# Up-projection of a convolutional feed-forward block: column blocks of 384 without overlap, edge taps from the preceding PSUM bank

## The chip, the core and the metric

The kernel runs on one core of one Trainium2 chip. The metric is the device time of one execution in microseconds (us). TensorE multiplies a loaded 128x128 weight tile by a moving operand of up to 512 columns and writes to PSUM, eight banks of 512 fp32 columns in each of 128 partitions. ScalarE, VectorE and GpSimd work on tiles beside it; each engine takes its own instructions strictly in order. The profile calls the engines PE, ACT, DVE and POOL, and SP is the engine that issues the transfers.

## The reference

Two layers, each a mixer (sliding-window or chunk-band attention) and a channel mixer, each closed by a layer norm. The change lies in the channel mixer, which the reference computes so:

```
def conv_ffn(h, prev, w_up, conv_w, conv_b, w_down):
    u = h @ w_up
    B, T, C = u.shape
    ...
    ue = jnp.concatenate([prev.astype(u.dtype), u], axis=1)
    y = conv_b
    for tap in range(CONV_W):
        y = y + conv_w[tap] * ue[:, tap:tap + T]
    a, g = jnp.split(y, 2, axis=-1)
    out = (jax.nn.gelu(g) * a) @ w_down
    return out, ue[:, T:]
```

There are 1024 prompt positions and 8 sample sequences of 16 positions, so 1152 positions in all, 1024 model channels and 2 x 2816 up-projected channels. The convolution is causal with three taps: a position needs the up-projected values of the two positions before it. For the prompt the first two positions see zeros; for a sample sequence they see rows of a stored state.

## The kernel before

All large products run in split fp32: each operand is a high and a low part, and three products (low by high, high by low, high by high) are summed in PSUM. H holds the modulated input of the channel mixer, transposed (channels on partitions, 1152 positions as columns), as a high and a low part; `wh` and `wl` are the two parts of a weight chunk.

The up-projection goes through 44 chunks of 128 channels a layer: chunk j of the value half (gg = 0) and chunk j + 22 of the gate half (gg = 1). Each chunk makes three position blocks, bi = 0, 1, 2. One block is 24 matmuls in line 266 (`mmT`: eight with `wl`, sixteen with `wh`) into one PSUM bank of the ring `ub` (banks 0, 1, 2). In the table `UB` (L995) block 0 takes columns 0 to 383, and blocks 1 and 2 take 388 columns that begin four columns before their own 384, so that all taps of a block find their inputs in the block's own bank.

`conv` (L972) then works on the bank: ScalarE writes bias plus the third tap to a tile `y` in SBUF (L975), and VectorE adds the other two taps straight from PSUM (L978), two instructions of 384 columns, or in block 2 two of 256 (prompt) and two on the sample part. GpSimd adds the sample state (L993). For the gate half follow gelu on ScalarE (L1022), the product with the value half on GpSimd (L1024) and the split of the result into X (ScalarE's cast in L151, VectorE's subtraction in L162). The down-projection (L1049, banks 3, 4, 5) multiplies two chunks of activations by two chunks of weights, and VectorE adds each result to `acc` (L1040). Up-blocks and down-blocks alternate.

The last chunk pair is made in `down_last` (L1053), block by block between the last down-projection rows, with `pregate` (L1104) before it: VectorE and GpSimd scale `acc` and add the residual (L1108, L1109).

Code order gives the dependences; a scheduler with a model of the engines' times then sets the order of the instructions on every engine at build time. Accesses of different engines to one PSUM bank are kept apart as whole banks, not as columns: a matmul group that writes bank 0 waits for every earlier reader of bank 0.

At the start of a channel mixer the last token tile, tile 7 of positions 896 to 1023, is still in its layer norm (`norm_tail`, L852): VectorE normalises it (L856), TensorE transposes it (L866, eight matmuls into banks 6 and 7), ScalarE applies the modulation (L878, eight copies), and ScalarE and VectorE split it into H. Block 2 needs this tile, blocks 0 and 1 do not. Tile names: F is a large SBUF arena (among others `y`, `acts`), C holds small per-position values, PS is PSUM.

Of the kernel before, what the change touches and what calls it, by code (L numbers as in the profile page):

```python
# [12 lines left out]
AF = mybir.ActivationFunctionType  # L13
# [6 lines left out]
NFF = 22  # L20
BLK = ((0, 384), (384, 384), (768, 384))
# [67 lines left out]
class Trunk:  # L89
# [693 lines left out]
    def ln_region(self):  # L783
        fa = Arena(self.F)
        x = fa.take(2048)
        self.xring = Ring([x[:, i * 1024 : i * 1024 + 1024] for i in range(2)])
        y = Arena(x)
        self.yg = y.ring(2, 384)
        self.at = y.ring(2, 384)
        for k in ("hf", "xr", "tmp"):  # L790
            setattr(self, k, fa.take(1024))
        self.E = fa.take(704)
        self.cw = fa.take(176)
        self.uo = [fa.take(198) for _ in range(2)]
        for k in ("gateS", "gateP", "lng", "lnb"):
            setattr(self, k, fa.take(1024))
        y = fa.take(1152)
        self.ya = Ring([y[:, i * 384 : i * 384 + 384] for i in range(3)])
        self.zt = fa.take(1024)
        assert fa.o <= self.NF, fa.o  # L800

    def ln_consts(self, l, i):
# [139 lines left out]
    def ffn(self, l, xsrc, xdst, affs):  # L942
        nc, I, O, H = self.nc, self.I, self.O, self.H
# [25 lines left out]
        x2b = self.x2p.tile([128, 768], F32R, name=f"x2ffn{l}", tag="x2b")  # L969
        aring = Ring([(x2.take(384), x2.take(384)) for _ in range(5)] + [(x2b[:, 0:384], x2b[:, 384:768])])  # L970

        def conv(ps, cc, bi, y):  # L972
            w = lambda i: cw[:, cc, i : i + 1]
            off = 0 if bi == 0 else 4
            nc.scalar.activation(y, ps[:, off : off + 384], AF.Identity, bias=w(3), scale=w(2))  # L975

            def tap(o, u, i):
                nc.vector.scalar_tensor_tensor(o, u, w(i), o, op0=ALU.mult, op1=ALU.add)  # L978

            if bi == 0:  # L980
                tap(y[:, 1:384], ps[:, 0:383], 1)
                tap(y[:, 2:384], ps[:, 0:382], 0)
            elif bi == 1:
                tap(y, ps[:, 3:387], 1)
                tap(y, ps[:, 2:386], 0)
            else:
                tap(y[:, 0:256], ps[:, 3:259], 1)
                tap(y[:, 0:256], ps[:, 2:258], 0)
                ys = y[:, 256:384].rearrange("p (s q) -> p s q", q=16)
                us = ps[:, 260:388].rearrange("p (s q) -> p s q", q=16)  # L990
                tap(ys[:, :, 1:16], us[:, :, 0:15], 1)
                tap(ys[:, :, 2:16], us[:, :, 0:14], 0)
                nc.gpsimd.tensor_add(ys[:, :, 0:2], ys[:, :, 0:2], E4[:, cc])  # L993

        UB = ((0, 384), (380, 388), (764, 388))  # L995

        acts = {}
        ya = {}

        def up(j, gg):  # L1000
            w = self.wload(I["wup"][l, j + 22 * gg])
            for bi in range(3):
                up_block(w, j, gg, bi)

        def up_block(w, j, gg, bi):
            cc = j + 22 * gg
            s0, n = UB[bi]
            ps = self.bank(ub.next())
            self.mmT(w, ps, s0, n)
            if gg == 0:  # L1010
                y = ya[bi] = self.ya.next()
            else:
                y = self.yg.next()
            conv(ps, cc, bi, y)
            if bi == 2:
                uo = self.uo[gg].rearrange("p (j s r) -> p j s r", s=9, r=2)
                src = ps[:, 258:402].rearrange("p (s q) -> p s q", q=16)[:, :, 0:2]
                nc.scalar.copy(uo[:, j % 11], src)
                if j % 11 == 10:
                    nc.sync.dma_start(O["conv"][l, gg, j // 11], self.uo[gg])  # L1020
            if gg == 1:
                nc.scalar.activation(y, y, AF.Gelu_apprx_tanh)  # L1022
                a = self.at.next()
                nc.gpsimd.tensor_mul(a, y, ya[bi])  # L1024
                h, lo = aring.next()
                self.split(a, h, lo, "a", "v")
                acts[(j, bi)] = (h, lo)
# [25 lines left out]
        def down_last():  # L1053

            js = (NFF - 2, NFF - 1)
            wu = [self.wload(I["wup"][l, NFF - 1 + 22 * gg]) for gg in range(2)]
            wr, wg = [], []
            for j, y in zip(js, (self.tmp, self.hf)):
                s = self.ws.next()
                wr.append(s)  # L1060
                nc.sync.dma_start(s, I["wdn"][l, j])
                nc.gpsimd.tensor_mul(y, s, self.gateP)
                wg.append(self.wring.next())
                self.split(y, *wg[-1], "a", "v")
            hfr = Ring([self.hf, self.tmp])
            for t in LO[l]:
                for bi in UP[l].get(t, ()):
                    for gg in range(2):
                        up_block(wu[gg], NFF - 1, gg, bi)
                    if bi == 2:  # L1070
                        w = [self.wring.next() for _ in range(2)]
                        for s, x in zip(wr, w):
                            self.split(s, *x, "a", "v")
                row = acc[:, t * 1024 : t * 1024 + 1024]
                sm = self.sm.next()
                for hf in range(2):
                    n = slice(hf * 512, hf * 512 + 512)
                    ps = dmm(js, wg if t < 8 else w, t, n)
                    if t == 8:
                        nc.vector.tensor_mul(self.tmp[:, n], ps, self.gateS[:, n])  # L1080
                        ps = self.tmp[:, n]
# [43 lines left out]
        self.step(0)  # L1125
        affs = affs()
        down_last()


# [214 lines left out]
```

## Time and profile before

| | |
|---|---|
| median of three runs | 2989.72 us (2989.35 to 2991.23) |
| the profiled execution | 2989.4 us |
| its span, first to last instruction | 2987.6 us |
| PE busy | 2858.9 us, 96% |
| PE weight loads | 2546.9 us, 85% |
| DVE busy | 1537.8 us, 51% |
| ACT busy | 1146.0 us, 38% |
| POOL busy | 913.8 us, 31% |
| channel mixer of layer 0, first up-block | at 516.81 us |
| channel mixer of layer 1, first up-block | at 2122.80 us |

A row of the timeline gives the start, the length, the engine, the line and the operation of a run of like instructions, and in brackets how long the engine had been idle and what it waited for. A matmul's own length holds its passage through the array, so that neighbours overlap: what a row of matmuls costs is read from its start to the start of the next row. Idle time of an engine that nothing waits for costs nothing.

### The profile page before, as it was taken

How to read it: one execution, taken by the hardware profiler on the slowest of the kernel's cores; microseconds unless marked ns; L12 is line 12 of the kernel's file. 1: busy time of each engine (PE TensorE's matmuls, PEld its weight loads, DVE VectorE, ACT ScalarE, POOL GpSimd, SP SyncE). 2: the span in 40 equal slices, each digit the busy share in tenths (PEclk: the TensorE clock that was granted, in tenths of full speed). 3: DMA queues.
4: the chain of work that ended last, by engine and by line, in shares of the span. 5: the costliest groups of instructions: out<-in, count | busy, mean ns of one | idle time of the engine just before them, and what ended most of it. 6: DMA issues, size and time to landing. Idle time of an engine off the chain costs nothing.

```text
span 2987.6 us, 43232 instructions
## 1 busy us (share of the span) xinstructions
PE 2858.9 (96%) x16582; PEld 2546.9 (85%) x16582; DVE 1537.8 (51%) x3416; ACT 1146.0 (38%) x2432; POOL 913.8 (31%) x661
## 2 busy tenths in 40 slices
PE   6999889999999999998999999989999999999996
PEld 4886668898888898997899888867899999999995
DVE  4365678424444344358412777766724444444468
ACT  2465644332222222224434666652442222222224
POOL 3122333323222222354551121221422222222253
PEclk8999999999999999999999999999999999999998
DMA  8545353622222312223785467673311111111121
GB/s 298 186 150 164 109 161 121 231 70 92 78 88 81 102 64 86 82 71 109 272 297 174 126 152 192 183 215 118 126 49 43 42 38 44 43 43 43 41 80 73
DMA packets 175967, 353.95 MB, mean 118 GB/s; under 512 B 34680, under 2 KB 91832, under 8 KB 175504
## 3 DMA queue, kind: packets, MB, share of 16 engines
q1 hardware_dynamic: 175760, 351.19, 36.6%
q8 instruction: 130, 2.13, 0.3%
q14 instruction: 77, 0.63, 0.1%
HBM read 285.22 MB, written 75.35 MB: 121 GB/s over the span
## 4 chain that ended last, share of the span: by engine, by line
PE 78%; DVE 8%; DMA 4%; ACT 3%; issue 2%; POOL 2%; SPq 0%; DVEq 0%; ACTq 0%; POOLq 0%
PE PS L266 45%; PE PS L1049 16%; PE PS L278 8%; PE PS L210 2%; PE PS L551 2%; PE PS L532 2%; PE PS L506 1%; DVE F L472 1%; PE PS L509 1%; DMA F<-in_adaw_dram 1%; DVE acc L1109 1%; DMA ws<-oN 1%; POOL wl L162 1%; DVE F L938 1%; DMA ws<-in_adaw_dram 1%
## 5 line engine op out<-in xcount | busy, mean ns | idle before, releaser
L266 PE MATMUL PS<-H,wh 128*128 128x384 f32 (+1 forms) x5472 | 1044.9, 338 | 0.0
L266 PEld LDWEIGHTS PS<-H,wh 128*128 128x128 f32 x5472 | 965.3, 188 | 17.7 <-issue 7.5
L162 POOL TENSOR_TENSOR wl<-ws,wh 128x1024 fp32r<-128x1024 f32 x167 | 405.5, 2433 | 743.4 <-ACT wh L151 696.9
L978 DVE SCALAR_TENSOR_TENSOR F<-PS,F 128x256 f32<-128x256 f32 (+2 forms) x704 | 353.0, 512 | 536.5 <-ACT F L975 523.2
L266 PE MATMUL PS<-H,wl 128*128 128x384 f32 (+1 forms) x2736 | 566.7, 344 | 21.1 <-POOL wl L162 9.4
L266 PEld LDWEIGHTS PS<-H,wl 128*128 128x128 f32 x2736 | 489.4, 190 | 53.3 <-issue 15.7
L975 ACT ACTIVATE F<-PS,F 128x384 f32<-128x384 f32 x264 | 177.5, 672 | 750.7 <-PE PS L266 749.3
L1049 PE MATMUL PS<-wh,X 128*128 128x512 f32 x1320 | 412.0, 394 | 9.6 <-DVE acc L1040 4.1
L1040 DVE TENSOR_TENSOR acc<-acc,PS 128x512 f32<-128x512 f32 x324 | 221.5, 686 | 270.9 <-PE PS L1049 270.3
L1024 POOL TENSOR_TENSOR F<-F 128x384 f32<-128x384 f32 x132 | 138.1, 1046 | 650.6 <-ACT F L1022 648.7
L1049 PEld LDWEIGHTS PS<-wh,X 128*128 128x128 f32 x1320 | 245.5, 188 | 63.0 <-issue 6.7
L151 ACT CAST wh<-ws 128x1024 fp32r<-128x1024 f32 x174 | 180.0, 1045 | 165.7 <-PE PS L1049 75.9
L1049 PE MATMUL PS<-wl,X 128*128 128x512 f32 x660 | 216.5, 393 | 0.0
L278 PE MATMUL PS<-wh,H 128*128 128x256 f32 (+1 forms) x936 | 171.2, 312 | 6.2 <-DVE H L162 5.4
L278 PEld LDWEIGHTS PS<-wh,H 128*128 128x128 f32 x936 | 136.0, 193 | 16.6 <-DVE H L162 6.0
L1049 PEld LDWEIGHTS PS<-wl,X 128*128 128x128 f32 x660 | 124.1, 188 | 28.1
L588 POOL TENSOR_TENSOR F<-F,x2att 64x512 f32<-64x512 f32 x62 | 79.4, 1280 | 216.2 <-DVE F L563 146.8
L162 DVE TENSOR_TENSOR X<-F,X 128x384 fp32r<-128x384 f32 x110 | 96.9, 881 | 88.9 <-ACT X L151 88.5
L532 PE MATMUL PS<-C,F 128*128 128x128 f32 x720 | 117.6, 284 | 16.0 <-DVE wh L538 7.6
L278 PE MATMUL PS<-x1att,H 128*128 128x512 f32 x504 | 131.9, 403 | 0.0
L1022 ACT ACTIVATE F<-F 128x384 f32<-128x384 f32 x132 | 69.2, 524 | 143.4 <-DVE F L978 129.2
L532 PEld LDWEIGHTS PS<-C,F 128*128 128x128 f32 x720 | 83.0, 143 | 37.9 <-DVE wh L538 11.0
(211 smaller groups left out, 3494.4 us busy)
## 6 DMA issues: line engine op xcount, KB each, us to landing
ws<-in_wup_dram SPq DMA_DIRECT2D x88, 512.0 KB
F<-in_adaw_dram SPq DMA_DIRECT2D x74, 512.0 KB
ws<-in_wdn_dram SPq DMA_DIRECT2D x44, 512.0 KB
ws<-in_adaw_dram SPq DMA_DIRECT2D x32, 512.0 KB
x1att<-kH SPq DMA_DIRECT2D x60, 256.0 KB
xd<-F SPq DMA_DIRECT2D x27, 512.0 KB
F<-xd SPq DMA_DIRECT2D x27, 512.0 KB
vH<-X SPq DMA_DIRECT2D x40, 256.0 KB
```

The lines of the kernel that those rows point to most:

```text
L151: nc.scalar.copy(out, in_)
L162: self.eng(el).tensor_sub(lo, src, hi.bitcast(F32))
L266: self.nc.tensor.matmul(out[:, 0:n], w[a][:, k * 128 : k * 128 + 128], H[:, p, k, s0 : s0 + n], start=i == 0, stop=i == 23)
L278: self.nc.tensor.matmul(out[:, 0:n], H[:, p, j * kn + k, t0 : t0 + 128], w[a][:, k * n : k * n + n], start=i == 0, stop=i == 23,)
L532: nc.tensor.transpose(t[:, m * 128 : m * 128 + 128], p[:, (kt - k0) * 128 : (kt - k0) * 128 + 128], self.ident)
L588: self.eng("v" if last else "p").tensor_mul(on[r, q], on[r, q], rb[r, :])
L975: nc.scalar.activation(y, ps[:, off : off + 384], AF.Identity, bias=w(3), scale=w(2))
L978: nc.vector.scalar_tensor_tensor(o, u, w(i), o, op0=ALU.mult, op1=ALU.add)
L1022: nc.scalar.activation(y, y, AF.Gelu_apprx_tanh)
L1024: nc.gpsimd.tensor_mul(a, y, ya[bi])
L1040: nc.vector.tensor_add(row[:, n], row[:, n], ps)
L1049: nc.tensor.matmul(ps, ac[m][p][:, cs], w[m][q][:, n], start=i == 0, stop=i == 5)
```

## The change

The blocks of the up-projection become the plain table of three times 384 columns. The two first columns of blocks 1 and 2 get the taps that cross the border by two small VectorE instructions (2 columns, then 1 column), which read the last two columns of the preceding block's PSUM bank. The wide taps start one and two columns into the block. The bank of a preceding block is therefore read by the next block's edge taps too. In `down_last`, where value and gate blocks alternate, ScalarE copies those two columns to SBUF (`halo`), and the edge taps read the copy.

```
-            off = 0 if bi == 0 else 4
-            nc.scalar.activation(y, ps[:, off : off + 384], AF.Identity, bias=w(3), scale=w(2))
+            nc.scalar.activation(y, ps[:, 0:384], AF.Identity, bias=w(3), scale=w(2))
...
-            if bi == 0:
-                tap(y[:, 1:384], ps[:, 0:383], 1)
-                tap(y[:, 2:384], ps[:, 0:382], 0)
-            elif bi == 1:
-                tap(y, ps[:, 3:387], 1)
-                tap(y, ps[:, 2:386], 0)
-            else:
-                tap(y[:, 0:256], ps[:, 3:259], 1)
-                tap(y[:, 0:256], ps[:, 2:258], 0)
+            if bi:
+                tap(y[:, 0:2], prev, 0)
+                tap(y[:, 0:1], prev[:, 1:2], 1)
+            n = 384 if bi < 2 else 256
+            tap(y[:, 1:n], ps[:, 0 : n - 1], 1)
+            tap(y[:, 2:n], ps[:, 0 : n - 2], 0)
+            if bi == 2:
...
-        UB = ((0, 384), (380, 388), (764, 388))
...
-            s0, n = UB[bi]
+            s0, n = BLK[bi]
             ps = self.bank(ub.next())
             self.mmT(w, ps, s0, n)
+            prev, last[gg] = last.get(gg), ps[:, 382:384]
...
-            conv(ps, cc, bi, y)
+            conv(ps, cc, bi, y, prev)
+            if keep and bi < 2:
+                nc.scalar.copy(self.halo[gg], ps[:, 382:384])
+                last[gg] = self.halo[gg]
```

By count: 4224 matmuls (88 chunks, two blocks, 24 each) go from 388 to 384 columns, their number stays; VectorE gets 352 instructions more (88 chunks, two blocks, two each), ScalarE 8 more. All lines behind the change move by one or two (L978 becomes L979, L866 becomes L867).

The scheduler also puts the work in another order. The first place is the start of the channel mixer of layer 1, TensorE. Before, from the second up-block of the first chunk on (value chunk 0, block 1; then gate chunk block 0; then the eight transposes of tile 7; gate block 1; block 0 of the next value chunk in two pieces, with value block 2 between them):

```order
L266 MATMUL PS<-H,wl 128x388 x8
L266 MATMUL PS<-H,wh 128x388 x16
L266 MATMUL PS<-H,wl 128x384 x8
L266 MATMUL PS<-H,wh 128x384 x16
L866 MATMUL PS<-C,F 128x128 x8
L266 MATMUL PS<-H,wl 128x388 x8
L266 MATMUL PS<-H,wh 128x388 x16
L266 MATMUL PS<-H,wl 128x384 x8
L266 MATMUL PS<-H,wh 128x384 x12
L266 MATMUL PS<-H,wl 128x388 x8
L266 MATMUL PS<-H,wh 128x388 x16
```

The same place of TensorE now, again from value block 1 on (then the transposes, gate block 0, value block 2, gate block 1, gate block 2):

```order
L266 MATMUL PS<-H,wl 128x384 x8
L266 MATMUL PS<-H,wh 128x384 x16
L867 MATMUL PS<-C,F 128x128 x8
L266 MATMUL PS<-H,wl 128x384 x8
L266 MATMUL PS<-H,wh 128x384 x16
L266 MATMUL PS<-H,wl 128x384 x8
L266 MATMUL PS<-H,wh 128x384 x16
L266 MATMUL PS<-H,wl 128x384 x8
L266 MATMUL PS<-H,wh 128x384 x16
L266 MATMUL PS<-H,wl 128x384 x8
L266 MATMUL PS<-H,wh 128x384 x16
```

The transposes of tile 7 have moved ahead of gate block 0, and gate block 1 and the next chunk's block 0, which stood before value block 2, stand behind it. Layer 0 starts in the same two ways.

The second place is the same start on VectorE. Before (the first row normalises tile 7; then the taps of value block 1, the closing sum of another token tile, the taps of gate block 0, the split of tile 7 into H, and taps of gate block 1 around a split of an activation into X):

```order
L856 TENSOR_SCALAR F<-F,C 128x1024
L978 SCALAR_TENSOR_TENSOR F<-PS,F 128x384 x2
L891 TENSOR_TENSOR F<-F 128x1024
L978 SCALAR_TENSOR_TENSOR F<-PS,F 128x383
L978 SCALAR_TENSOR_TENSOR F<-PS,F 128x382
L162 TENSOR_TENSOR H<-F,H 128x8x128
L978 SCALAR_TENSOR_TENSOR F<-PS,F 128x384
L162 TENSOR_TENSOR X_73<-F,X_73 128x384
L978 SCALAR_TENSOR_TENSOR F<-PS,F 128x384
```

The same place of VectorE now; the rows of 2 columns and of 1 column are the edge taps, the first pair reading bank 0 for value block 1, the second reading bank 1 for value block 2:

```order
L857 TENSOR_SCALAR F<-F,C 128x1024
L979 SCALAR_TENSOR_TENSOR F<-PS,F 128x2
L979 SCALAR_TENSOR_TENSOR F<-PS,F 128x1
L979 SCALAR_TENSOR_TENSOR F<-PS,F 128x383
L979 SCALAR_TENSOR_TENSOR F<-PS,F 128x382
L892 TENSOR_TENSOR F<-F 128x1024
L162 TENSOR_TENSOR H<-F,H 128x8x128
L979 SCALAR_TENSOR_TENSOR F<-PS,F 128x383
L979 SCALAR_TENSOR_TENSOR F<-PS,F 128x382
L162 TENSOR_TENSOR X_73<-F,X_73 128x384
L979 SCALAR_TENSOR_TENSOR F<-PS,F 128x2
L979 SCALAR_TENSOR_TENSOR F<-PS,F 128x1
```

Gate block 0 writes bank 0 and so stands behind the first pair, which stands behind the normalising of tile 7; gate block 1 writes bank 1 and stands behind the second pair, which stands behind the split of gate block 0's activation.

The third place is VectorE at the end of layer 1's channel mixer, where the last rows of `pregate` meet the split of a down-projection weight and the taps of the last but one value chunk's gate block 2. Before:

```order
L162 TENSOR_TENSOR X_73<-F,X_73 128x384
L1040 TENSOR_TENSOR acc_17141<-acc_17141,PS 128x512
L1109 SCALAR_TENSOR_TENSOR acc_17141<-F,acc_17141 128x1024
L1040 TENSOR_TENSOR acc_17141<-acc_17141,PS 128x512 x3
L1109 SCALAR_TENSOR_TENSOR acc_17141<-F,acc_17141 128x1024
L162 TENSOR_TENSOR wl<-F,wh 128x1024
L978 SCALAR_TENSOR_TENSOR F<-PS,F 128x256
```

And now:

```order
L162 TENSOR_TENSOR X_73<-F,X_73 128x384
L1042 TENSOR_TENSOR acc_17321<-acc_17321,PS 128x512
L1111 SCALAR_TENSOR_TENSOR acc_17321<-F,acc_17321 128x1024
L1042 TENSOR_TENSOR acc_17321<-acc_17321,PS 128x512
L162 TENSOR_TENSOR wl<-F,wh 128x1024
L979 SCALAR_TENSOR_TENSOR F<-PS,F 128x2
L979 SCALAR_TENSOR_TENSOR F<-PS,F 128x1
L979 SCALAR_TENSOR_TENSOR F<-PS,F 128x255
```

One row of `pregate` now stands behind the weight split instead of ahead of it, and the edge taps that free the preceding bank stand directly behind that split.

## Rows read from the trace of the kernel before

**Rows 1.** The page: busy time by engine; granted TensorE clock in 40 slices.
```profile
PE 2858.9 (96%) x16582; PEld 2546.9 (85%) x16582; DVE 1537.8 (51%) x3416; ACT 1146.0 (38%) x2432; POOL 913.8 (31%) x661
...
PEclk8999999999999999999999999999999999999998
```

**Rows 2.** The page: the chain that ended last, by engine.
```profile
PE 78%; DVE 8%; DMA 4%; ACT 3%; issue 2%; POOL 2%; SPq 0%; DVEq 0%; ACTq 0%; POOLq 0%
```

**Rows 3.** Windows: length, then busy time of PE, PEld, DVE, ACT, POOL, clock, DMA.
```profile
515.00:1300.00 785.00, 782.37 (x4137) 696.40 (x4136) 313.40 (x544) 219.04 (x370) 223.30 (x173) 1.00 0.29 98
...
2900.00:2987.60 87.60, 60.89 (x290) 53.21 (x288) 73.82 (x152) 36.58 (x60) 33.70 (x18) 0.89 0.22 81
```

**Rows 4.** Timeline of PE in attention: three blocks of 384 in a row.
```profile
101.89 1.55 PE L266 MATMUL PS<-H,wl 128*128 128x384 f32 x8
...
114.38 0.22 PE L506 MATMUL PS<-x1att 128*128 128x128 f32 x1
```

**Rows 5.** Timeline of PE: one chunk's blocks 0, 1, 2, then down-projection.
```profile
2857.22 1.57 PE L266 MATMUL PS<-H,wl 128*128 128x384 f32 x8
...
2861.41 1.58 PE L266 MATMUL PS<-H,wl 128*128 128x388 f32 x8
2862.83 2.99 PE L266 MATMUL PS<-H,wh 128*128 128x388 f32 x16
2865.66 1.57 PE L266 MATMUL PS<-H,wl 128*128 128x388 f32 x8
...
2869.90 0.62 PE L1049 MATMUL PS<-wh,X 128*128 128x512 f32 x2
2870.36 0.62 PE L1049 MATMUL PS<-wl,X 128*128 128x512 f32 x2
```

**Rows 6.** DVE by line and form: busy time, mean ns of one.
```profile
L978 DVE SCALAR_TENSOR_TENSOR F<-PS,F 128x383 f32<-128x383 f32 x88 | 54.1, 615 | 195.6 <-ACT F L975 195.5
L978 DVE SCALAR_TENSOR_TENSOR F<-PS,F 128x120 f32<-128x120 f32 x88 | 29.3, 333 | 0.0
```

**Rows 7.** Timeline of PE at the start of layer 1's channel mixer.
```profile
2133.96 1.65 PE L266 MATMUL PS<-H,wl 128*128 128x384 f32 x8 [1.68 <-DVE F L978]
...
2138.22 1.04 PE L866 MATMUL PS<-C,F 128*128 128x128 f32 x8
2139.01 1.66 PE L266 MATMUL PS<-H,wl 128*128 128x388 f32 x8
```

**Rows 8.** Timeline of DVE at the same start.
```profile
2130.75 0.15 DVE L829 TENSOR_SCALAR C<-C 128x1 f32<-128x1 f32 x1
...
2134.41 0.81 DVE L856 TENSOR_SCALAR F<-F,C 128x1024 f32<-128x1024 f32 x1
```

**Rows 9.** Timeline of ACT at the same start.
```profile
2138.47 0.67 ACT L975 ACTIVATE F<-PS,F 128x384 f32<-128x384 f32 x1 [5.48 <-PE PS L266]
2139.04 2.90 ACT L878 ACTIVATE F<-PS,C 128x128 f32<-128x128 f32 x8
2141.96 1.28 ACT L1022 ACT_TABLE_LOAD   x1
...
2145.19 0.50 ACT L151 CAST X<-F 128x384 fp32r<-128x384 f32 x1
```

**Rows 10.** Timeline of POOL at the same start.
```profile
2143.91 1.01 POOL L1024 TENSOR_TENSOR F<-F 128x384 f32<-128x384 f32 x1 [6.21 <-ACT F L1022]
```

**Rows 11.** Timeline of PE at the start of layer 0's channel mixer.
```profile
527.09 1.65 PE L266 MATMUL PS<-H,wl 128*128 128x384 f32 x8 [0.80 <-DVE F L978]
...
558.70 1.05 PE L210 MATMUL PS<-F,C 128*32 128x512 f32 x4 [1.83 <-DMA F<-in_adaw_dram]
```

**Rows 12.** Timeline of DVE at the same start of layer 0.
```profile
528.55 0.81 DVE L856 TENSOR_SCALAR F<-F,C 128x1024 f32<-128x1024 f32 x1
```

**Rows 13.** Waits of PE from 2890 us on: total, times, longest.
```profile
PE PS L1049 <- DVE C L1085: 3.2, 2, 2.3
PE PS L266 <- POOL wl L162: 2.3, 1, 2.3
PE PS L1049 <- DVE acc L1040: 2.1, 2, 1.8
```

More of the change, by code (lines that the diff above doesn't have):

```diff
@@ L799, in ln_region @@
         self.zt = fa.take(1024)
+        self.halo = [fa.take(2) for _ in range(2)]
         assert fa.o <= self.NF, fa.o
@@ L970, in ffn, with conv @@
         aring = Ring([(x2.take(384), x2.take(384)) for _ in range(5)] + [(x2b[:, 0:384], x2b[:, 384:768])])
-        def conv(ps, cc, bi, y):
+        def conv(ps, cc, bi, y, prev):
             w = lambda i: cw[:, cc, i : i + 1]
-            off = 0 if bi == 0 else 4
-            nc.scalar.activation(y, ps[:, off : off + 384], AF.Identity, bias=w(3), scale=w(2))
+            nc.scalar.activation(y, ps[:, 0:384], AF.Identity, bias=w(3), scale=w(2))
             def tap(o, u, i):
                 nc.vector.scalar_tensor_tensor(o, u, w(i), o, op0=ALU.mult, op1=ALU.add)
-            if bi == 0:
-                tap(y[:, 1:384], ps[:, 0:383], 1)
-                tap(y[:, 2:384], ps[:, 0:382], 0)
-            elif bi == 1:
-                tap(y, ps[:, 3:387], 1)
-                tap(y, ps[:, 2:386], 0)
-            else:
-                tap(y[:, 0:256], ps[:, 3:259], 1)
-                tap(y[:, 0:256], ps[:, 2:258], 0)
+            if bi:
[5 more added lines that the diff above has]
+            if bi == 2:
                 ys = y[:, 256:384].rearrange("p (s q) -> p s q", q=16)
-                us = ps[:, 260:388].rearrange("p (s q) -> p s q", q=16)
+                us = ps[:, 256:384].rearrange("p (s q) -> p s q", q=16)
                 tap(ys[:, :, 1:16], us[:, :, 0:15], 1)
@@ L993, in conv @@
                 nc.gpsimd.tensor_add(ys[:, :, 0:2], ys[:, :, 0:2], E4[:, cc])
-        UB = ((0, 384), (380, 388), (764, 388))
         acts = {}
         ya = {}
+        last = {}
         def up(j, gg):
@@ L1003, in up, with up_block @@
                 up_block(w, j, gg, bi)
-        def up_block(w, j, gg, bi):
+        def up_block(w, j, gg, bi, keep=False):
             cc = j + 22 * gg
-            s0, n = UB[bi]
+            s0, n = BLK[bi]
             ps = self.bank(ub.next())
             self.mmT(w, ps, s0, n)
+            prev, last[gg] = last.get(gg), ps[:, 382:384]
             if gg == 0:
@@ L1013, in up_block @@
                 y = self.yg.next()
-            conv(ps, cc, bi, y)
+            conv(ps, cc, bi, y, prev)
+            if keep and bi < 2:
+                nc.scalar.copy(self.halo[gg], ps[:, 382:384])
+                last[gg] = self.halo[gg]
             if bi == 2:
                 uo = self.uo[gg].rearrange("p (j s r) -> p j s r", s=9, r=2)
-                src = ps[:, 258:402].rearrange("p (s q) -> p s q", q=16)[:, :, 0:2]
+                src = ps[:, 254:398].rearrange("p (s q) -> p s q", q=16)[:, :, 0:2]
                 nc.scalar.copy(uo[:, j % 11], src)
@@ L1068, in down_last @@
                     for gg in range(2):
-                        up_block(wu[gg], NFF - 1, gg, bi)
+                        up_block(wu[gg], NFF - 1, gg, bi, True)
                     if bi == 2:
```

## The prediction

> **What bounds the kernel now.** I read the page first, then the windows, then timelines. TensorE is busy 96% of the span [rows 1] and has 78% of the chain that ended last [rows 2]. Inside the first channel mixer it is busy 782.37 of 785 us, at a granted clock of 1.00 of full speed, which is the 2.4 GHz level [rows 3]. There everything that TensorE no longer has to stream shortens the kernel, and everything that other engines get on top is free as long as it frees PSUM banks in time. The exceptions are the few places where TensorE waits: the starts of the two channel mixers [rows 7, 11] and their ends, where the window from 2900 us on holds only 60.89 us of TensorE work in 87.6 [rows 3].
>
> **What the narrower blocks give.** 88 chunks have two blocks each that go from 388 to 384 columns: 176 blocks of 24 matmuls, 4224 matmuls. A block's price is start to start. Blocks of 388: 2861.41 to 2865.66 is 4.25 us, 2865.66 to 2869.90 is 4.24 us, so 176.9 ns a matmul [rows 5]. Three blocks of 384 in a row, in attention, take 101.89 to 114.38, 12.49 us or 4.163 us a block, 173.5 ns a matmul [rows 4]. The difference is 0.082 us a block, times 176 is 14.4 us. Block 0 of the same chunk, already 384 wide, takes 4.19 us behind a 388 block [rows 5], slower than in attention; if the new neighbours cure that too, 88 x 0.027 = 2.4 us come on top, 16.8 in all. If instead 4.19 is what every 384 block in this place costs, the gain is 0.055 x 176 = 9.7 us. Lowest bound: columns alone. A 512-column matmul takes 2869.90 to 2870.36 for two, 230 ns [rows 5], so 56.5 ns over 128 columns, 0.44 ns a column, 1.77 ns for four, 7.5 us in all. I take 13.5 us, about the middle of 9.7 and 16.8, near the row for blocks of 384 in a row, since that is what most blocks become.
>
> The rows say that the four columns cost 3.4 ns where their share by column would be 1.8. The Trainium skill, page "TensorE: Matmul & The Clock Gate", section "Back-to-back issue gap", gives a warm gap of N/2.4 + 2.5 ns, by which four columns are 1.67 ns and the whole step 7.0 us. This trace differs for 388 columns (164.2 by the rule, 176.9 measured), so I give the rule's outcome only a small chance, as a rival.
>
> **What the edge taps cost.** A tap of 383 columns takes 615 ns, one of 120 takes 333 [rows 6]: 1.07 ns a column, and at 2 columns 333 - 118 x 1.07 = 207 ns. The smallest VectorE instruction at hand takes 0.15 us [rows 8], a lower bound; 0.33 is the upper one. With 0.21 us, 352 of them are 74 us more work for VectorE, 51% to about 53% of the span. Beside TensorE this is hidden; what matters is when a bank comes free.
>
> In the steady part a bank was free after its own block's taps; now blocks 0 and 1 hold theirs until the next block's edge taps. Walk it in [rows 5]: block 1 ends on TensorE at 2862.83 + 2.99 = 2865.82, ScalarE takes 0.04 + 0.67 us [rows 9], the two edge taps 0.42, so bank 0 is free at 2866.95. It is wanted at the earliest when block 2 ends, 2869.90. The slack is 2.95 us. ScalarE and VectorE may be late by that much before TensorE feels it, so I cost the steady part at nothing. Without that cover each of the 176 blocks would pay (rival below).
>
> **Start of layer 1.** Gate block 0 writes bank 0, which value block 1's edge taps read last, and the order now puts the transposes of tile 7 ahead of it. Tile 7 is normalised at 2134.41 + 0.81 = 2135.22 [rows 8]; the edge taps end 0.4 later, hidden by the transposes. These take 2138.22 to 2139.01, 0.79 us [rows 7], so gate block 0 starts at 2136.01 in place of 2133.96. It takes 2133.96 to 2138.22, 4.26, and ends at 2140.27; before, the same work (block and transposes) was done at 2139.01. Loss 1.26 us. Value block 2 follows at once to 2144.4. Gate block 1 now needs the second pair of edge taps, and these stand behind a long queue: ScalarE reads gate block 0 (2140.3 to 2141.0), two taps of 0.6 (2142.2), table load and gelu (2141.96 to 2143.91 before, 1.95 us [rows 9, 10]: 2144.15), GpSimd's product 1.01 [rows 10] (2145.15), the cast of 0.50 (2145.65), ScalarE's 0.67 for value block 2 (2146.3), the edge taps 0.42 (2146.75). TensorE stands idle 2146.75 - 2144.4 = 2.35 us. Before, gate block 1 and the next block 0 filled this time. Together 3.6 us.
>
> **Start of layer 0.** The same steps: tile 7 normalised at 528.55 + 0.81 = 529.36 [rows 12], transposes to 530.15, gate block 0 to 534.41; before, the same work ended at 527.09 + 4.26 + 0.79 = 532.14 [rows 11]. Loss 2.27. The gap before gate block 1 is again 2.35, and value block 2 may wait for tile 7's split (eight copies of 2.90 in all, then cast and subtraction), for which I add 0.5, an estimate between 0 and 1. That is 5.1, of which the next wait of TensorE, 1.83 us for a weight transfer at 558.70 [rows 11], gives back 1.8, since it comes later anyway. 3.3 us remain. Bounds of both starts together: 0, if the queues run faster than I walk them, to 10.
>
> **The ends.** TensorE loses 3.2 + 2.3 + 2.1 us to waits in layer 1 [rows 13], and layer 0 has the same pattern. The order moves one `pregate` row behind the weight split, which lets the split and the taps behind it start earlier, and may take some of the 2.3. Against it the gate block's bank is freed by edge taps behind that split, and four extra edge taps (0.84 us) stand in the last chain of each layer. ScalarE's eight copies lie beside other work. I take a loss of 1.0 for both ends, between a gain of 4 and a loss of 5, half of the waits of two ends and the extra taps either way.
>
> **Sum.** -13.5 + 3.6 + 3.3 + 1.0 = -5.6 us. The profiled execution took 2989.4 us, 1.8 more than its span, so 2983.8; the median shown is 0.3 higher, hence 2984.
>
> **The rivals.**
>
> *The starts cost little.* If ScalarE and VectorE get through their queues before TensorE needs the banks, or what is lost is given back by later waits, only cadence counts: 2989.7 - 13.5 + 1 = 2977, at best some us below. For it speaks that layer 0 has a later wait; against it that layer 1 has no later wait until its end.
>
> *Columns alone count.* The gain is 7.0 to 7.5 us, the starts cost 6.9 and the ends 1: 2990, no change. Against it: 4.163 against 4.245 us in the trace of one execution.
>
> *The bank hold stalls the steady part (slower).* The two engines work in order; when a ScalarE cast or a VectorE split stands ahead of the next block's ScalarE step and edge taps, the slack of 2.95 us is eaten. In the walk above one such queue (gelu, product, cast) came to 4.4 us between a block's first taps and the edge taps behind it, more than the slack. Break-even is 5.6/176 = 0.032 us a block. If one of ten chunks pays 2 us in each layer, 9 x 2 = 18, and the time is 2984 + 18 = 3002. For it speaks the rule of whole banks; against it that in the steady part gelu follows a block's taps without a table load, and blocks are spread by down-projections. The Trainium skill, page "PSUM — Partial Sum Buffer", section "PSUM bank collisions raise a hardware error", says that a different address of the same bank still collides, so the two columns hold the whole bank; it agrees with the order, and no row here shows what it costs.
>
> **Chances.** Forecast 0.50 (2980 to 2990), cheap starts 0.24, columns alone 0.10, steady stalls 0.16. A measurement of this kernel can tell about 0.2%, 6 us, from no change, and my forecast of 5.7 us under the median lies at this border. Faster: half of the forecast's chance, nearly all of the second: 0.47. Slower: 0.14 of the last and 0.01 of the forecast: 0.15. The same: 0.38. The range: with two in ten outside, 2975 to 2996, from cheap starts with an end that gains to stalls on a few chunks.
>
> **What would show it.** Line 266 should show only 384 columns and a block of 4.16 to 4.19 us start to start in the steady part; that is the step on which most hangs. At both starts a wait of TensorE of 2 to 3 us ahead of gate block 1, released by line 979 on VectorE. Edge taps of 0.15 to 0.33 us, 352 of them. No waits of line 266 for line 979 between the starts and the ends: if these are there in number, the slower rival is right. If block pitch falls by only 0.04 us, columns alone count.

## The result and the profile after

| | before | after |
|---|---|---|
| median | 2991.09 us (7 runs) | 3000.31 us (7 runs, 2993.87 to 3005.95) |
| ratio | | 1.0027, 95% interval 1.0014 to 1.0040 |
| profiled execution, span | 2987.6 us | 2992.1 us |
| mean granted clock of it | 0.984 | 0.982 |
| PE busy | 2858.9 us | 2852.6 us |
| DVE busy, instructions | 1537.8 us, 3416 | 1615.9 us, 3768 |

The kernel became slower by 0.27%, some 8 us (the two medians lie 9.2 us apart), where 5.7 us of gain were forecast. The profiled execution is the fastest of its seven; their times go with their mean granted clock, from 2993.87 us at 0.982 to 3005.95 at 0.975. The two profiles differ by 4.5 us of span, so a reading of them accounts for half of the loss; the rest lies in executions that were not profiled.

**The narrower blocks did what was forecast.** Timeline of PE after the start of layer 1, three blocks in a row (start, length, engine, line, operation, and the idle time before):

```profile
2155.57 1.55 PE L266 MATMUL PS<-H,wl 128*128 128x384 f32 x8
...
2159.73 1.55 PE L266 MATMUL PS<-H,wl 128*128 128x384 f32 x8
...
2163.89 1.55 PE L266 MATMUL PS<-H,wl 128*128 128x384 f32 x8
```

4.16 us a block, start to start, where [rows 5] had 4.25 and 4.24. TensorE's busy time fell although its clock was lower.

**The edge taps cost what was forecast for them.** VectorE by form (busy time, mean ns of one, idle time before):

```profile
L979 DVE SCALAR_TENSOR_TENSOR F<-PS,F 128x2 f32<-128x2 f32 x168 | 36.9, 219 | 308.8 <-ACT F L976 307.8
L979 DVE SCALAR_TENSOR_TENSOR F<-PS,F 128x1 f32<-128x1 f32 x168 | 36.7, 218 | 5.7
```

0.22 us each, against an estimate of 0.21.

**The starts cost twice what was forecast.** Timeline of PE at the start of layer 1; it answers to [rows 7]:

```profile
2136.08 1.38 PE L867 MATMUL PS<-C,F 128*128 128x128 f32 x8 [2.92 <-DVE F L857]
2137.11 2.91 PE L266 MATMUL PS<-H,wl 128*128 128x384 f32 x8
2139.82 3.13 PE L266 MATMUL PS<-H,wh 128*128 128x384 f32 x16
2142.79 1.55 PE L266 MATMUL PS<-H,wl 128*128 128x384 f32 x8
2144.17 2.94 PE L266 MATMUL PS<-H,wh 128*128 128x384 f32 x16
2149.71 2.38 PE L266 MATMUL PS<-H,wl 128*128 128x384 f32 x8 [2.60 <-DVE F L979]
2151.88 3.85 PE L266 MATMUL PS<-H,wh 128*128 128x384 f32 x16
```

Both waits are where the walk had put them: 2.92 us ahead of the transposes, and 2.60 ahead of gate block 1 (2.35 forecast), released by line 979. But gate block 0 then takes 2137.11 to 2142.79, 5.68 us, and gate block 1 takes 2149.71 to 2155.57, 5.86 us, where a block that follows a wait took 4.26 [rows 7]. Windows of 5 us show the clock there (length; busy time of PE, PEld, DVE, ACT, POOL; granted clock; DMA share; GB/s):

```profile
2130.00:2135.00 5.00, 3.16 (x19) 2.84 (x17) 4.88 (x10) 0.87 (x2) 2.35 (x3) 1.00 0.64 222
2135.00:2140.00 5.00, 3.92 (x17) 3.93 (x18) 3.68 (x7) 3.20 (x9) 2.36 (x1) 0.67 0.07 21
2140.00:2145.00 5.00, 5.00 (x30) 5.00 (x29) 2.45 (x3) 1.43 (x2) 0.00 (x0) 0.99 0.95 320
2145.00:2150.00 5.00, 2.40 (x15) 2.08 (x14) 1.35 (x5) 3.75 (x5) 0.99 (x1) 1.00 0.46 186
2150.00:2155.00 5.00, 5.00 (x21) 5.00 (x21) 1.11 (x4) 0.26 (x2) 2.56 (x2) 0.66 0.27 102
```

Behind each wait the granted clock fell from its upper level (2.4 GHz, 1.00) to its lower one (1.2 GHz) for about 3 us: 0.67 and 0.66 in the mean over the window. Each fall costs about 1.5 us on top of the wait (5.68 and 5.86 against 4.26). Layer 0 shows the same twice:

```profile
531.17 1.09 PE L867 MATMUL PS<-C,F 128*128 128x128 f32 x8 [3.20 <-DVE F L857]
532.01 2.53 PE L266 MATMUL PS<-H,wl 128*128 128x384 f32 x8
...
537.83 1.55 PE L266 MATMUL PS<-H,wl 128*128 128x384 f32 x8
...
544.75 1.79 PE L266 MATMUL PS<-H,wl 128*128 128x384 f32 x8 [2.59 <-DVE F L979]
...
550.59 1.55 PE L266 MATMUL PS<-H,wl 128*128 128x384 f32 x8
```

**The end of layer 1 got a longer wait.** Waits of TensorE there, which answer to [rows 13]; before, the wait for line 1085 at the corresponding point was 0.89 us:

```profile
2917.27 0.50 PE L1051 MATMUL PS<-wh,X 128*128 128x512 f32 x1 [2.33 <-DVE acc L1042]
2918.88 2.90 PE L266 MATMUL PS<-H,wl 128*128 128x384 f32 x8 [1.11 <-DVE F L979]
2957.63 0.73 PE L1051 MATMUL PS<-wh,X 128*128 128x512 f32 x2 [3.27 <-DVE C L1087]
2963.72 0.50 PE L1051 MATMUL PS<-wh,X 128*128 128x512 f32 x1 [2.25 <-DVE C L1087]
```

VectorE and GpSimd ahead of the 3.27 us, first VectorE, then GpSimd:

```profile
2949.62 1.52 DVE L979 SCALAR_TENSOR_TENSOR F<-F 128x2 f32<-128x2 f32 x1 [0.19 <-ACT F L976]
...
2954.17 2.74 DVE L850 TENSOR_TENSOR acc<-acc,F 128x1024 f32<-128x1024 f32 x1
```

```profile
2948.72 2.41 POOL L849 TENSOR_TENSOR acc<-acc,F 128x1024 f32<-128x1024 f32 x1
2953.28 2.54 POOL L849 TENSOR_TENSOR acc<-acc,F 128x1024 f32<-128x1024 f32 x1 [2.15 <-ACT acc L848]
```

An edge tap on the copy in SBUF took 1.52 us for two columns and ended (2951.14) right behind GpSimd's instruction (2948.72 + 2.41 = 2951.13). The addition of the norm's bias in line 850, whose inputs lie in SBUF too, then took 2.74 us beside GpSimd's second instruction. In the kernel before the same addition ran ahead of that instruction:

```profile
2952.28 1.20 DVE L849 TENSOR_TENSOR acc<-acc,F 128x1024 f32<-128x1024 f32 x1
```

Together that is 1.3 and 1.5 us of delay, and TensorE's wait grew by 2.38.

The two waits at 2917 and 2919 are no loss. The kernel before waits 0.30, 1.77 and 2.26 us from 2900 to 2920, 4.33 in all against 2.33 + 1.11 = 3.44 now, and the block behind these waits is slow in both kernels.

Where the time went can be read step by step. Both programs issue 16582 TensorE instructions, so the start of the n-th one tells how late a kernel is against before. The stages below are cut at instructions 2750, 3250, 7250, 12150, 12500, 16250 and the last (475.3, 573.4, 1334.8, 2109.9, 2174.7, 2890.6 and 2968.0 us in the kernel before); each number is the us lost (+) or gained (-) in that stage against the profile of before. The stage between 7250 and 12150 holds the end of layer 0 and the attention of layer 1. The kernels named in the rows are described in the next section.

| profile of | start 0 | steady 0 | end 0, attention 1 | start 1 | steady 1 | end 1 |
|---|---|---|---|---|---|---|
| after | +6.6 | -7.1 | -1.1 | +7.6 | -5.0 | +1.1 |
| after_again | +5.1 | -7.1 | +2.1 | +7.3 | -5.0 | +2.3 |
| halo_first | +0.7 | -7.5 | +5.9 | +4.0 | -5.3 | +2.5 |
| no_edge | -0.8 | -5.3 | -0.8 | 0.0 | -5.7 | +0.8 |
| hold_only | +6.9 | -2.2 | +0.6 | +6.9 | +0.4 | -0.8 |
| overlap_first | -1.2 | -7.5 | +3.2 | +1.6 | -5.3 | +2.5 |
| overlap_both | -0.8 | -7.5 | +1.2 | +2.8 | -5.3 | -1.3 |
| overlap_last | +6.6 | -7.1 | +2.6 | +7.8 | -5.0 | -0.1 |

Attention before the first stage differs by up to 5 us from execution to execution, and the third column carries such differences too.

### The profile page after: what moved, and what is told of

It reads as the page before. It is cut to its first block, busy times and chain, and to the rows that moved or that the text cites. A ratio compares the mean times of both kernels' runs of the same rounds, so it can differ in the third digit from the quotient of the medians.

```text
span 2992.1 us, 43590 instructions
## 1 busy us (share of the span) xinstructions
PE 2852.6 (95%) x16582; PEld 2539.0 (85%) x16582; DVE 1615.9 (54%) x3768; ACT 1145.4 (38%) x2440; POOL 918.5 (31%) x661
## 4 chain that ended last, share of the span: by engine, by line
PE 79%; DVE 10%; DMA 4%; ACT 3%; POOL 2%; issue 2%; SPq 0%; DVEq 0%; POOLq 0%; ACTq 0%
PE PS L266 46%; PE PS L1051 16%; PE PS L278 8%; PE PS L551 2%; PE PS L210 2%; PE PS L532 2%; PE PS L506 1%; DVE F L472 1%; POOL acc L1110 1%; PE PS L509 1%; DVE acc L1111 1%; DMA ws<-in_wo_dram 1%; DVE C L826 1%; DMA ws<-oN 1%; DVE F L939 0%
## 5 line engine op out<-in xcount | busy, mean ns | idle before, releaser
L266 PE MATMUL PS<-H,wh 128*128 128x384 f32 x5472 | 1039.8, 337 | 0.0
L979 DVE SCALAR_TENSOR_TENSOR F<-PS,F 128x382 f32<-128x382 f32 (+7 forms) x1040 | 410.2, 415 | 508.1 <-ACT F L976 492.7
L266 PE MATMUL PS<-H,wl 128*128 128x384 f32 x2736 | 567.4, 343 | 22.8 <-DVE H L153 8.8
L162 DVE TENSOR_TENSOR X<-F,X 128x384 fp32r<-128x384 f32 x110 | 127.9, 1163 | 84.8 <-ACT X L151 84.3
```

The lines of the kernel that those rows point to most:

```text
L162: self.eng(el).tensor_sub(lo, src, hi.bitcast(F32))
L266: self.nc.tensor.matmul(out[:, 0:n], w[a][:, k * 128 : k * 128 + 128], H[:, p, k, s0 : s0 + n], start=i == 0, stop=i == 23)
```

## The experiments

The theory after the result: the gain of the narrower blocks is there; the two starts lose about 14 us by waits and by the falls of the clock behind them; the ends lose some more. Rivals: the hold of the banks or VectorE's added work costs in the steady part, or the four columns give less than thought.

**after_again**, the changed kernel unchanged. 

> The changed kernel once more, to see its spread and a second profile. Theory (starts): the two starts of the channel mixers cost 6.6 and 7.6 us, by two waits of TensorE each and by the granted clock falling to its lower level behind each wait; the rest gains about 15 us and the ends lose about 3. Median 2994 to 3003 us, with windows of granted clock under 0.9 right behind the waits at both starts. Rival (steady part): the edge taps hold banks in the steady part, then the profile shows further waits of line 266 for line 979 between the starts and the ends.

2999.15 us, ratio 1.0030 (1.0019 to 1.0041); a second profile with 2994.9 us of span at clock 0.979. The starts cost +5.1 and +7.3 us. In layer 0 gate block 0 ran at full speed this time (4.27 us) behind a wait of 3.20, so one of the four falls is missing. In the steady part of neither profile does a wait of line 266 for line 979 appear: TensorE's waits in the profile of after (total, times, longest) have four of them, which the timelines place at the two starts (2.59, 2.60) and the two ends (1.11, 1.11), and after_again has four at the same places:

```profile
PE PS L266 <- DVE F L979: 7.4, 4, 2.6
```

**halo_first**, ScalarE's copies also in the first chunk pair. 

> The changed kernel, but in the first value chunk and the first gate chunk of each layer ScalarE copies the two edge columns to SBUF as it does in the last chunk, so no bank is held there by the next block's edge taps; TensorE's order at the starts is then that of the kernel before. Theory (starts): the start costs of about 14 us go, the time is 2976 to 2982 us. Rival (steady part holds banks or VectorE is overloaded): the starts are a minor part, the time stays at 2990 or above. Rival (columns give less than thought): 2984 to 2990.

```
-                up_block(w, j, gg, bi)
+                up_block(w, j, gg, bi, j == 0)
```

2989.03 us, ratio 0.9987 (0.9978 to 0.9997): 10 us faster than the changed kernel, but short of the expected 2976 to 2982. The start of layer 0 is repaired (+0.7). In layer 1 TensorE still waited, now for the copy (L1015), and the clock fell:

```profile
2134.42 2.25 PE L266 MATMUL PS<-H,wl 128*128 128x384 f32 x8 [1.79 <-ACT F L1015]
2136.47 3.93 PE L266 MATMUL PS<-H,wh 128*128 128x384 f32 x16
```

The block takes 5.82 us to 2140.24, behind a wait of 1.79; before, the wait of 1.68 at the same place left the clock alone [rows 7]. So it is not the wait alone that decides, and a little more of it can cost 1.6 us. The stage holds a second loss: at 2172.40 TensorE waits 1.27 us for line 979, in the second chunk pair, whose edge taps read PSUM.

**no_edge**, no edge taps. 

> The changed kernel without the edge taps: the two border columns of blocks 1 and 2 lack the taps that cross the border; the halo copies of the last chunk stay. No bank is held for the next block and VectorE has 352 instructions less. Theory (starts): about as fast as the version with copies in the first chunk, 2973 to 2980 us, since in the steady part the edge taps cost TensorE nothing. Rival (steady part): faster than the version with copies in the first chunk by 5 us or more.

```
-            if bi:
-                tap(y[:, 0:2], prev, 0)
-                tap(y[:, 0:1], prev[:, 1:2], 1)
```

2980.21 us, ratio 0.9963 (0.9951 to 0.9975). It lies 9 us below halo_first, which fits the rival of its expectation; the table shows where: 4 us at the start of layer 1, 1.7 in its end and 6.7 in the stage between, which also differs between executions of one kernel, and nothing in the steady parts (-5.3 and -5.7 against -7.5 and -5.3). So the rival's number came out, but not its place.

**hold_only**, the blocks of before, with two small instructions that read the preceding bank. 

> The kernel before, with blocks of 388 columns and overlap, plus two small VectorE instructions for blocks 1 and 2 of all chunks but the last pair that read columns 382 and 383 of the preceding bank and write a tile nobody reads: the hold of the bank alone, without the narrower blocks. TensorE's order at the starts is then that of the changed kernel. Theory (starts): 14 us slower than before, 3001 to 3008 us, all of it at the two starts. Rival (the cost lies in the narrower blocks or at the ends): within 4 us of before.

```
+            if bi and prev is not None:
+                k = self.halo[cc // 22]
+                nc.vector.scalar_tensor_tensor(k, prev, w(0), y[:, 0:2], op0=ALU.mult, op1=ALU.add)
+                nc.vector.scalar_tensor_tensor(k[:, 0:1], prev[:, 1:2], w(1), y[:, 0:1], op0=ALU.mult, op1=ALU.add)
```

3003.67 us, ratio 1.0036 (1.0024 to 1.0048), as the theory had it: +6.9 at either start, and in the steady part of layer 1 +0.4. The hold, with the two small instructions that make it and the order that follows from it, makes the starts' loss, without one narrower block. Why the steady part of layer 0 is 2.2 us faster than before in this profile stays open.

**overlap_first**, **overlap_both**, **overlap_last**: the 388-column blocks of before stay in the first chunk pair, in the first and the last, or in the last. The edit, with the set that differs (`j == 0`; `j in (0, NFF - 1)`; `j == NFF - 1`):

```
+            ov = OVER(j)
+            keep = keep and not ov
-            s0, n = BLK[bi]
+            s0, n = UB[bi] if ov else BLK[bi]
...
+            off = 4 if ov and bi else 0
```

> The changed kernel, but the first value chunk and first gate chunk of each layer keep the 388-column blocks with overlap; no bank is held there and ScalarE copies nothing. TensorE's order at the starts is that of the kernel before. Theory (starts, with the clock falling behind waits): both starts cost nothing against the kernel before, the rest gains 14, the ends lose 3: 2980 to 2984 us, and at both starts a granted clock of 1.00. Rival (edge taps cost in the steady part, which would explain why the version with copies stood at 2989 and the one without edge taps at 2980): 2987 to 2992.

> As the version with overlap in the first chunk, and the last chunk pair of each layer keeps 388 columns with overlap too, so no copies and no edge taps stand in the ends. Theory: the ends lose nothing more, 2976 to 2981 us, the fastest of all versions that compute everything. Rival (the ends are not touched by it): as the version with overlap in the first chunk alone, within 1.5 us.

> The changed kernel, but only the last chunk pair of each layer keeps 388 columns with overlap. Theory: the starts cost 14 us as in the changed kernel, the ends 3 us less: 2994 to 2998 us. Rival (the ends make up most of the loss): below 2990 us.

In this order: 2989.16 us, ratio 0.9990 (0.9980 to 1.0000); 2980.20 us, ratio 0.9962 (0.9950 to 0.9975); 2995.00 us, ratio 1.0009 (0.9999 to 1.0019). Against the median of after_again the starts are worth 10.0 us (2999.15 - 2989.16), or 14.8 with the ends repaired (2995.00 - 2980.20); the ends are worth 4.2 us (2999.15 - 2995.00), or 9.0 with the starts repaired (2989.16 - 2980.20). The first expectation put the ends at 3 and missed by 5 us; its rival's number came out, but overlap_both has the same edge taps in the steady part and stands at 2980. The profiled execution of overlap_first is the fastest of its eleven, 4.9 us under their median, so the profiles show less of the ends than the medians. overlap_both is 0.38% faster than before with all values computed. TensorE's waits in its end of layer 1 are back to those of before for the last chunk:

```profile
2947.11 0.74 PE L1061 MATMUL PS<-wh,X 128*128 128x512 f32 x2 [0.88 <-DVE C L1097]
2952.86 0.50 PE L1061 MATMUL PS<-wh,X 128*128 128x512 f32 x1 [2.24 <-DVE C L1097]
```

At the second last gate block it waits as the changed kernel does, and the block behind is slow as well, so that place is not what the repair of the ends gives back:

```profile
2908.66 0.50 PE L1061 MATMUL PS<-wh,X 128*128 128x512 f32 x1 [2.34 <-DVE acc L1052]
2910.27 2.58 PE L266 MATMUL PS<-H,wl 128*128 128x384 f32 x8 [1.11 <-DVE F L980]
```

Its start of layer 1 still loses 2.8 us in the profile. Part of that is the wait that halo_first has too, in the second chunk pair, where edge taps read PSUM:

```profile
2168.32 1.69 PE L266 MATMUL PS<-H,wl 128*128 128x384 f32 x8 [1.27 <-DVE F L980]
```

**fill**, work for TensorE ahead of gate block 1. 

> The changed kernel with 14 extra matmuls of 384 columns in the first value chunk's block 2, into a bank that is not in use yet and that nobody reads, so that TensorE has work in most of the time before gate block 1 (2.4 us of added work). Theory (a wait of TensorE of over 2 us is followed by a fall of the granted clock, and that makes gate block 1 take 5.8 in place of 4.2 us): the wait before gate block 1 falls from 2.6 to about 1 us or less, and gate block 1 runs at 4.2 us; in all no slower than the changed kernel although 4.8 us of work are added in two layers. Rival (gate block 1 is slow for another reason, its operands or its bank): it stays at 5.8 us.

```
+                if j == 0 and gg == 0 and bi == 2:
+                    fill = self.bank(5)
+                    for k in range(14):
+                        nc.tensor.matmul(fill[:, 0:384], w[0][:, 0:128], H[:, 0, 0, 768:1152], start=True, stop=True)
```

3000.28 us, ratio 1.0032 (1.0020 to 1.0045): as slow as the changed kernel, with 4.8 us more work. Timeline of PE, layer 1 (L1005 is the added work):

```profile
2157.61 2.59 PE L1005 MATMUL PS<-H,wh 128*128 128x384 f32 x14
2160.03 2.94 PE L266 MATMUL PS<-H,wh 128*128 128x384 f32 x16
2164.24 1.68 PE L266 MATMUL PS<-H,wl 128*128 128x384 f32 x8 [1.27 <-DVE F L979]
2165.76 2.93 PE L266 MATMUL PS<-H,wh 128*128 128x384 f32 x16
2168.53 1.55 PE L266 MATMUL PS<-H,wl 128*128 128x384 f32 x8
```

The wait is 1.27 us, and gate block 1, with the same operands, bank and releaser, takes 4.29 us (2164.24 to 2168.53) instead of 5.86. Layer 0 shows the same 4.29. So the slow block is the clock's doing. Gate block 0 stands behind the longer wait still. In layer 1 it takes 5.39 us (2150.83 to 2156.22, clock 0.67), in layer 0 4.27:

```profile
537.12 1.09 PE L867 MATMUL PS<-C,F 128*128 128x128 f32 x8 [3.20 <-DVE F L857]
537.97 1.66 PE L266 MATMUL PS<-H,wl 128*128 128x384 f32 x8
542.24 1.55 PE L266 MATMUL PS<-H,wl 128*128 128x384 f32 x8
```

**vec_norm**, the last layer's norm multiplication on VectorE instead of GpSimd. 

> The changed kernel, but the multiplication by the norm's weight in the last layer's end runs on VectorE instead of GpSimd, so that GpSimd has hardly an instruction running when the last chunk's edge taps read SBUF. Theory (the edge tap that reads SBUF waits for GpSimd there): that tap takes 0.22 us in place of 1.5, and TensorE's wait of 3.3 us ahead of the last down-projection rows falls to 1 to 2 us; the time falls by 1 to 4 us against the changed kernel, 2995 to 2999. Rival (the wait comes from the count of instructions in the chain of the end, not from GpSimd): the wait stays at 3 us or more.

```
-            nc.gpsimd.tensor_mul(x, x, self.lng)
+            nc.vector.tensor_mul(x, x, self.lng)
```

2998.22 us, ratio 1.0026 (1.0017 to 1.0036), not clearly faster than the changed kernel. The mechanism held: the slow edge tap takes 0.20 us, the addition in line 850 takes 1.22, and the wait of 3.27 falls to 0.34. The time did not follow: later waits came, and the three below make 5.69 us where the changed kernel's two made 5.52. That VectorE's added work makes the later ones is likely, but not shown:

```profile
2959.79 0.72 PE L1051 MATMUL PS<-wh,X 128*128 128x512 f32 x2 [0.34 <-DVE C L1087]
2964.81 0.49 PE L1051 MATMUL PS<-wh,X 128*128 128x512 f32 x1 [1.49 <-DVE C L1087]
2969.17 0.80 PE L1051 MATMUL PS<-wh,x2ffn 128*128 128x512 f32 x1 [3.86 <-DVE x2ffn L162]
```

**halo_all**, ScalarE's copies in all chunks. 

> The changed kernel with ScalarE's copies of the two edge columns in all chunks: no edge tap reads PSUM, no bank is held for the next block, 176 copies on ScalarE. Theory (an edge tap that reads SBUF and starts while GpSimd is in an instruction ends with that instruction; those that read PSUM do not): tens of edge taps of 0.3 to 2.4 us; the starts cost as in the version with copies in the first chunk alone, the ends too: 2986 to 2993 us. Rival (it is the read of PSUM that costs, in the steady part): 2983 or below.

```
-                up_block(w, j, gg, bi)
+                up_block(w, j, gg, bi, True)
```

2986.71 us, ratio 0.9981 (0.9972 to 0.9991). VectorE by form:

```profile
L979 DVE SCALAR_TENSOR_TENSOR F<-F 128x1 f32<-128x1 f32 x176 | 68.0, 386 | 5.8
L979 DVE SCALAR_TENSOR_TENSOR F<-F 128x2 f32<-128x2 f32 x176 | 63.6, 362 | 252.4 <-ACT F L976 251.1 <-ACT F L1015 0.2
```

Edge taps from SBUF take 0.37 us in the mean, up to 2.43, from PSUM 0.22. Steady parts: -6.3 and -5.2, so these longer taps are hidden there too. The time lies in the theory's range.

**double_taps** and **double_mid**, overlap_both with each pair of edge taps followed by two more that read the same columns into a tile nobody reads, in all other chunks, or only in layer 1 and 16 of 22 chunk pairs. The lines of double_mid:

```
+                    for _ in range(2 if l == 1 and 2 <= cc % 22 <= 17 else 0):
+                        k = self.halo[cc // 22]
+                        nc.vector.scalar_tensor_tensor(k, prev, w(0), y[:, 0:2], op0=ALU.mult, op1=ALU.add)
```

> The version with overlap in the first and last chunk pair, and in all other chunks two more small VectorE instructions behind each pair of edge taps, which read the same two columns of the preceding bank and write a tile nobody reads: VectorE's added work and the hold of the bank are doubled (320 more instructions of about 0.22 us, 70 us in all). Theory (in the steady part the edge taps lie beside TensorE's work, with 2.95 us of slack): within 1.5 us of the version without them, 2979 to 2983 us. Rival (the steady part pays for edge taps): slower by 4 us or more.

> The version with overlap in the first and last chunk pair, with two more small VectorE instructions behind each pair of edge taps (reading the preceding bank, writing a tile nobody reads) only in layer 1 and only in 16 of its 22 chunk pairs, so that starts, ends and all of layer 0 keep their order: 128 more instructions, 28 us of VectorE. It is the cleaner form of the doubling in all chunks, which also changed the order of layer 0 and its end. Theory (steady edge taps lie beside TensorE's work): within 2 us of 2980.2 us, and TensorE has no wait for these lines in the steady part of layer 1. Rival (the steady part pays about the instructions' own time): 2990 us or more.

double_taps: 2997.39 us, ratio 1.0015 (1.0006 to 1.0024), 17 us more than overlap_both and a clear miss. Against overlap_both its profile loses 6.3 us in the steady part of layer 0, 4.2 in the stage behind it, 1.1 in the steady part of layer 1 and 4.5 in the end. In the steady part of layer 0 TensorE waits for no edge tap. The edit had given TensorE another order there: the modulation matmuls (L210) stand in groups of 2 to 12, where overlap_both has mostly eight. In the stretch from 600 to 1320 us one of them takes 172.6 ns from its start to the next start, where overlap_both has 142.4; for 216 of them that is 6.5 us, the whole loss of this stage. At the end of layer 0 one hold did cost, 6.39 us (L992 is the added read), and at the end of layer 1 another 6.42:

```profile
1363.06 2.90 PE L266 MATMUL PS<-H,wl 128*128 128x384 f32 x8 [6.39 <-DVE F L992]
```

double_mid changes TensorE's order in the steady part of layer 1 alone: 2983.80 us, ratio 0.9971 (0.9960 to 0.9982), 3.6 us above overlap_both, beyond the expected 2 and far from the rival's 2990; the intervals of the two ratios overlap. Its steady part of layer 1 gains 4.5 us instead of 5.3, and TensorE has no wait for an edge tap there that overlap_both does not have. So 28 us of added edge work and a doubled hold cost some 0.8 us in the profile. That steady edge taps cost nothing at all is not shown; a microsecond or two for all of them stays possible.

## Why the prediction was wrong, by its steps

**Cadence, -13.5: right.** Blocks take 4.16 us. From 2200 to 2840 us, layer 1, the mean from one matmul of line 266 to the next falls from 176.8 ns (388 columns) and 174.8 (384) to 174.1. The measured worth: overlap_both, which narrows 80 of 88 chunks, is 12.6 us under before in medians (2992.85 - 2980.20), 13.9 for all 88. The cheaper rival, 7 us by columns alone, is out. That 13.5 fits so closely is partly luck: it was the middle between two readings of the rows. The Trainium skill, page "TensorE: Matmul & The Clock Gate", section "Back-to-back issue gap", gives N/2.4 + 2.5 ns as the gap of an isolated matmul of N columns at the upper level of the clock; an estimate from it is 1.67 ns for four columns and 7.0 us for the whole step. The measurement decides against it here, where a block of 388 costs 0.08 us more than one of 384.

**Edge taps, steady part at nothing: right within the 1 to 2 us that the doubling leaves open.**

**Starts, +6.9: the place and the waits right, the clock left out.** This is the step that failed. In layer 0 the waits grew from 0.80 to 3.20 + 2.59, by 5.0 us (2.27 + 2.35 + 0.5 forecast), of which the transfer's 1.83 came back as forecast. In layer 1 they grew from 1.68 to 0.51 + 2.92 + 2.60, by 4.35 (3.6 forecast). On top, in the profile of after, come four blocks at the lower clock: 5.82 and 5.84 in layer 0, 5.68 and 5.86 in layer 1, against 4.26 each, 6.2 us that no term of the sum had. Waits of 7.5 net and these 6.2 make 13.7; the profile lost 14.2 and the second one 12.4.

The sign stood in the trace of before. The same wait of 2.26 us ahead of the same block, in the ends of layer 0 and of layer 1:

```profile
1362.28 1.68 PE L266 MATMUL PS<-H,wl 128*128 128x384 f32 x8 [2.26 <-POOL wl L162]
1363.80 2.93 PE L266 MATMUL PS<-H,wh 128*128 128x384 f32 x16
...
2917.32 2.77 PE L266 MATMUL PS<-H,wl 128*128 128x384 f32 x8 [2.26 <-POOL wl L162]
2919.89 3.45 PE L266 MATMUL PS<-H,wh 128*128 128x384 f32 x16
```

In layer 0 the block runs at full speed, in layer 1 eight matmuls take 2.57 us and not 1.52, and the next sixteen 3.29 and not 2.77: 1.6 us, the price of a fall. The prediction read the idle time in brackets and not the length of the rows behind it.

**Ends, +1.0 (bounds -4 to +5): mis-sized.** By the medians, versions that keep the overlap in the last chunk pair lie 4.2 and 9.0 us under those that do not. The profiles show about half of the larger figure. In layer 1 the end costs 1.1, 2.3, 2.5 and 2.5 us in after, after_again, halo_first and overlap_first, and -1.3 and -0.1 in overlap_both and overlap_last. In layer 0, from instruction 7250 to 8121, the same kernels have -0.8, 1.8, 3.9 and 2.8 against 0.3 and 0.2. For layer 1 the cause is shown: VectorE's instructions on SBUF that wait for GpSimd, and the wait of 3.27 us instead of 0.89. "ScalarE's copies lie beside other work" was true of the copies; what reads them was not looked at. For layer 0, and for what the medians have beyond the profiles, it stays open.

Two numbers of the working are off. Half of the waits of two ends, of 7.6 us each, would be 7.6 us, where the bounds of -4 and +5 go by half of one end's; the bounds were too narrow by their own rule. VectorE's share comes to 54% and not 53 (54% measured).

**Sum.** Forecast were -13.5 + 6.9 + 1.0. By the medians the starts and the ends together cost 19.0 us (2999.15 - 2980.20), 10.0 to 14.8 of it at the starts, and overlap_both stands 12.6 under before (2992.85 - 2980.20): some 6 us slower in these series, 8 in the first. The slower rival had the sign and the wrong place: TensorE does not stall in the steady part, and the bank hold costs where the queues ahead of the edge taps are long.

## What to carry to other kernels

Price a new wait of TensorE with the block that follows it as well: where a wait of 2 to 3 us appears in a stretch that was dense, look whether rows of the trace behind waits of that length run at half speed, and add that (here 1.5 us each, four times in one profile and three times in the other). A second reader of a PSUM bank costs at most a microsecond or two in all where the slack is 3 us, and the queue ahead of it where engines are still busy with the stage before; keeping the old scheme for the first and last chunk pair gave back nearly all of it (2980 us). Do not take the reader of a copy to be free when the copy lies in SBUF and GpSimd works.

## What the runs showed of the hardware

**The granted clock falls behind short waits, not every time.** Falls stood behind waits of 1.79 (halo_first), 2.60, 2.92 and 3.20 us (after). In the kernel before the wait of 1.68 had none, and of two waits of 2.26 one had a fall and one had none. In fill gate block 0 ran at full speed (4.27 us, 537.97 to 542.24) right behind a wait of 3.20, and so it did in after_again. What decides is not shown by these runs. Mean clock and time of single runs of one kernel go together (0.982 and 2993.87 us, 0.975 and 3005.95).

**VectorE on SBUF waits for GpSimd, VectorE on PSUM does not.** In the profile of after, 46 edge taps that read PSUM started while GpSimd was in an instruction; the longest took 222 ns. The one SBUF edge tap that did took 1523 ns and ended 18 ns after GpSimd's instruction; in halo_first there were three such, of 2326, 2292 and 1522 ns, each ending 15 to 18 ns behind GpSimd's. In halo_all 38 SBUF edge taps started so: 35 ended 12 to 23 ns behind GpSimd's instruction and took up to 2348 ns, three kept their 219 to 222 ns. The Trainium skill, page "SBUF — State Buffer", section "🔬 SBUF: two separate sides", says that a VectorE operation with two SBUF inputs and a GpSimd operation that reads SBUF lock one port pair for a whole instruction, and whoever comes second waits. The numbers agree but for those three: the tap from PSUM has one input in SBUF, the tap from SBUF has two.

**Four columns cost about 3 ns a matmul.** Matmuls of 388 columns in the kernel before take 176.8 ns start to start in the steady part of layer 1, those of 384 columns in the kernel after 174.1, a step of 2.7 where 0.44 ns a column would give 1.8.
